# Three opening weight pieces on GpSimd's queue, and block-sum scalings behind the first eight tiles

## The chip, the cores and the metric

The kernel runs on one core of a Trainium2 chip. A core has engines that work side by side, each through its own list of instructions in order: TensorE (PE, the matmuls, with its weight loads listed as PEld), VectorE (DVE), ScalarE (ACT), GpSimd (POOL) and SyncE (SP), which here only issues transfers. A transfer (DMA) is issued by an engine's queue and carried out by the core's 16 DMA engines; a semaphore tells when it has landed. The metric is the device time of one execution in microseconds (us).

## The reference

One layer of a hybrid decoder: 16 learned meta tokens stand ahead of 2048 tokens of width 1024, all are RMS-normalised, projected by one matrix of 1024 x 4096 into eight groups, and go through a gated short convolution and a retention; an output projection, the residual and a last norm follow.

```python
def mixer_layer(h, norm_g, w_in, conv_w, ret_norm_g, w_out, pos):
    hn = rms_norm(h, norm_g)
    proj = jnp.einsum('bld,de->ble', hn, w_in)
    cx, cb, cc, cg, q, k, v, rg = jnp.split(proj, N_PROJ, axis=-1)
    conv_out = short_conv_branch(cx, cb, cc, conv_w) * jax.nn.silu(cg)
...
    ret = head_group_norm(retention_chunkwise(qf, kf, vf), ret_norm_g)
    ret_out = ret.astype(h.dtype) * jax.nn.silu(rg)
    mixed = jnp.concatenate([conv_out, ret_out], axis=-1)
    return h + jnp.einsum('ble,ed->bld', mixed, w_out)
```

## The kernel before

**Products in parts.** Matmuls run on rounded float32 (`F32R`). Each operand is split into a rounded high part (`mh`, `wh`, made by ScalarE) and the rest as a low part (`ml`, `wl`, made by VectorE), and each product is three matmuls: high by high, high by low, low by high. `split` (line 108) does this; with a scale, for the x tiles and their norm gain, ScalarE's line is 115 and VectorE's 116, without one they are 112 and 113.

**Tiles.** x comes transposed in tiles of 128 x 512 (`xT`, 256 KB each). For the first half of the sequence there are two groups `j` of 512 tokens, with eight tiles `k` of 128 model dimensions each. A set of weights is four blocks of 128 x 512: `n = 0, 1` make one output, `n = 2, 3` the other, and even `n` serve tiles 0 to 3, odd `n` tiles 4 to 7. Within a block, columns `128 k` to `128 (k+1)` belong to tile `k`. Later units use a scheme with seven products on sums of blocks (`quad`, line 236); the first unit is done plainly (`quad_plain`, matmuls on line 293): two outputs, three matmuls, so six matmuls to a tile of x.

**The opening.** Blocks 0 and 2 of the first set are cut in two `PIECES`: the first 128 columns, which tile 0 needs, and the other 384. Before, the two first pieces (64 KB each) were issued by ScalarE's queue on line 942, behind the small `gain`, and the two others (192 KB each) by SP's queue on line 990, behind x tile 0. Their casts and low parts are lines 999 and 1000. `moving` (line 167) loads and splits the x tiles in order and calls what stands for `(j, k)` in its dictionary `after`: `begin(0)` behind tile 0, `begin(1)` behind tile 3, which loads blocks 1 and 3 whole (line 498 issues them), and `normalise_meta` behind tile 7.

**Block sums.** The seven-product scheme wants sums of x blocks. `block_sums` starts with a scaling of one block by the gain on ScalarE (line 192), four in this stage, and goes on with VectorE's line 189 and a subtraction on GpSimd.

**Identity.** `make_identity` writes a 128 x 128 identity with two GpSimd instructions (`masks.py:197` and `199`), among the first of that engine. Its first reader is VectorE's line 314.

**What sets the order.** A planner takes the program, simulates it, and writes each engine's list. `tc.issue_after(ins)` makes instructions of the block that are on the same engine as `ins` stand behind it in that engine's list. It orders the list alone; nothing waits for `ins` to end. Waits come from data and from buffers.

Of the kernel before, what the change touches and what calls it, by code (L numbers as in the profile page):

```python
# [8 lines left out]
F32 = mybir.dt.float32  # L9
# [4 lines left out]
ALU = mybir.AluOpType  # L14
# [5 lines left out]
KT = D // P  # L20
NG = 4
# [5 lines left out]
KH = KT // 2  # L27
# [5 lines left out]
BLOCK = ((0, 7), (1, 5))  # L33
FIRST_W, PLAIN_W, B12 = 2, 3, 4
# [44 lines left out]
def hybrid_trunk(ctx: ExitStack, tc: tile.TileContext, t, out: bass.AP, chunk_decay):  # L79
# [5 lines left out]
    nc = tc.nc  # L85
# [18 lines left out]
    def brief(name="b"):  # L104
        return sb.tile([P, HB + 128], F32, name=name, tag="b", bufs=BRIEF)[:, :HB]

    lowered, fifth = [None], [None]

    def split(hi, lo, src, scale=None, eng=nc.vector):

        if scale is None:
            nc.scalar.copy(out=hi, in_=src)  # L112
            lowered[0] = eng.tensor_tensor(out=lo, in0=src, in1=hi.bitcast(F32), op=ALU.subtract)  # L113
            return
        nc.scalar.mul(hi, src, scale)  # L115
        nc.vector.scalar_tensor_tensor(
            out=lo, in0=src, scalar=scale, in1=hi.bitcast(F32), op0=ALU.mult, op1=ALU.subtract
        )
# [37 lines left out]
    def operand(i, kt):  # L156
        slot = B12 if i == 7 else i
        hi = sb.tile([P, HB], F32R, name=f"mh{i}{kt}", tag=f"mh{slot}{kt}", bufs=1)
        lo = sb.tile([P, HB], F32R, name=f"ml{i}{kt}", tag=f"ml{slot}{kt}", bufs=1)
        return hi, lo  # L160

    def parts(m, i, kt, src, factor=None):
        hi, lo = operand(i, kt)
        split(hi, lo, src, factor)
        m[i].append((hi, lo))

    def moving(load, scale=None, after={}):


        m = [[] for _ in range(8)]  # L170
        blocks = []
        for j in range(2):
            for half in range(2):
                for kt in range(KH):
                    k = half * KH + kt
                    blocks.append(load(k, j))
                    parts(m, BLOCK[half][j], kt, blocks[-1], scale(k) if scale else None)
                    after.get((j, k), lambda: None)()
        return m, blocks

# [165 lines left out]
    ident = const.tile([P, P], F32, name="ident")  # L346
# [67 lines left out]
    def gain_of(k):  # L414
        return gain[:, k : k + 1]

    def load_x(r):
        def load(k, j):
            a = gen("x")[:, :HB]
            nc.sync.dma_start(a, t["xT"][r, j, k])  # L420
            return a

        return load
# [514 lines left out]

    PIECES = slice(0, P), slice(P, HB)
    opening = {n: raw() for n in (0, 2)}  # L940
    for n, a in opening.items():
        nc.scalar.dma_start(a[:, PIECES[0]], t["w_in"][2 * NG, n][:, PIECES[0]])
    make_identity(nc, ident)
    nc.gpsimd.memset(ones, 1.0)
    nc.gpsimd.memset(neg_half, -0.5)
    nc.vector.tensor_copy(out=ones_r, in_=ones)
# [24 lines left out]
    for r in range(NR):  # L971
        f = factors[r]
        rot_t = sb.tile([P, 2, BLK], F32, name="rot_t", tag="rot_t", bufs=1)
        p0 = NMETA + r * BLK

        def load_tables():
            nc.sync.dma_start(rot_t, t["rot"][:, :, p0 : p0 + BLK])

        if r == 0:
            w = [None] * 4  # L980
            loads = w_loads(2 * NG)

            def begin(half):
                if half:
                    for n in (1, 3):
                        w[n] = plain_part(n, loads[n], FIRST_W)
                    return
                for n, a in opening.items():
                    w[n] = a, operand(FIRST_W, n)
                    nc.sync.dma_start(a[:, PIECES[1]], t["w_in"][2 * NG, n][:, PIECES[1]])  # L990
                done = []
                for cs in PIECES:
                    with ExitStack() as behind:
                        for ins in done:
                            behind.enter_context(tc.issue_after(ins.ins))
                        for n, a in opening.items():
                            hi, lo = w[n][1]
                            done = [
                                nc.scalar.copy(out=hi[:, cs], in_=a[:, cs]),
                                nc.vector.tensor_tensor(  # L1000
                                    out=lo[:, cs], in0=a[:, cs], in1=hi[:, cs].bitcast(F32), op=ALU.subtract
                                ),
                            ]

            m, b = moving(
                load_x(r), gain_of, {(0, 0): lambda: begin(0), (0, KH - 1): lambda: begin(1), (0, KT - 1): normalise_meta}
            )
            first = [[p for a, p in w]]
            blocks = None, meta_products([a for a, p in w])
            first.append(plain_parts(w_loads(2 * NG + 1)))  # L1010
            load_tables()
            nc.sync.dma_start(cols, t["cols"])
            t3 = [a[:, i * HB : (i + 1) * HB] for a in (row_tile("t3", 1) for _ in range(2)) for i in range(2)]
            t1 = [brief("t1") if n < BRIEF else sb.tile([P, HB], F32, name="t1", tag="tc", bufs=COPIES) for n in range(KH)]
            for kt in range(KH):
                b11, b21, b12, b22 = (b[n * KH + kt] for n in range(4))
                block_sums(b11, b12, b22, b21, t1[kt], t3[kt], gain_of(kt), gain_of(KH + kt), nc.gpsimd)
                parts(m, 2, kt, b22)
                parts(m, 6, kt, b21)
            for _ in row_factors(0, f):  # L1020
                pass
            nc.sync.dma_start(causal, t["causal"])
            nc.sync.dma_start(conv_w, t["conv_w"])
            nc.sync.dma_start(ret_g, t["ret_norm_g"])

            def late_parts():
                for i, held in ((3, t1), (4, t3)):
                    for kt in range(KH):
                        parts(m, i, kt, held[kt])

            between = (), idle, idle
            later = prepare(load_x(1), sums_x, gain_of)
        else:
            m, b = moving(load_x(r), gain_of)
            first = [plain_parts(w_loads(0))]
            load_tables()
            prepared(m, sums_x, (1, 3))

            def rest_of_sums():
                prepared(m, sums_x, (0, 2))  # L1040
                with tc.issue_after(loaded[0].ins):
                    kept.pop()()

            between = (), rest_of_sums, idle
            blocks = None, None
            later = prepare(load_w_out, sums_w)
        factors_ahead[0] = row_factors(r + 1, factors[r + 1]) if r < NR - 1 else iter(())
        units = UNITS[r]
        turning = None
        special = (first, between)  # L1050
        for n, unit in enumerate(units):
            following = units[n + 1] if n + 1 < len(units) else None
            rest = lambda: ahead(r, following, early=n == 0)
            if r + n == 0:
                blocks, completion = group_plain(unit - NG, m, f, blocks[1], first, late_parts, rest)
                special = (), completion
            elif unit < NG:
                if turning is None:
                    turning = [row_tile(name, 1 - r) for name in ("apart", "across")]
                sums = later if unit in MAKES_SUMS[r] else iter(())  # L1060
                blocks = head(unit, r, m, rot_t, f, turning, blocks, rest, sums, *(special if unit == 0 else ()))
            else:
                if r == NR - 1 and following is None:
                    lent = sb.tile([P, 2, BLK], F32, name="held", tag="rot_t", bufs=1)
                    areas = [lent[:, 0], lent[:, 1], row_tile("held", 0), row_tile("held", 0)]
                    for i, a in enumerate(areas):
                        for j in range(2):
                            n, kt = 2 * (i // 2), i % 2 * 2 + j
                            held[n, kt] = a[:, j * HB : (j + 1) * HB]
                            nc.sync.dma_start(held[n, kt], sums_w[n, kt])  # L1070
                blocks = conv_group(unit - NG, r, m, f, blocks, rest, FACTOR_STEPS.get(unit, ()) if r == 0 else (), r == 0 and following is None)
                if unit in MAKES_SUMS[r]:
                    with tc.issue_after(taken[0].ins):
                        next(later, None)

    m, b = moving(load_w_out)
# [42 lines left out]
```

## Time and profile before

| what | us |
|---|---|
| median of 3 runs | 870.76 (869.86 to 871.42) |
| profiled execution | 871.07 |
| its span | 869.3 |
| TensorE busy | 857.9 |
| VectorE busy | 722.5 |
| ScalarE busy | 497.9 |
| GpSimd busy | 396.6 |

The span is the profiled part of an execution; 1.8 us of the execution lie outside it. Busy times are of the whole span. A timeline row gives the start in us from the span's beginning, the duration, the engine, the line, the operation, what it writes and reads, its shapes and count, and in brackets how long the engine stood idle before it and what ended that. A row with a count merges neighbours of one kind. Names with a q, such as SPq, are the queue of that engine, which issues transfers.

### The profile page before, as it was taken

The numbers are of one execution on the slowest core, as the hardware profiler recorded it, in microseconds if no ns is written. First come the engines' busy times: TensorE is split into PE (matmuls) and PEld (weight loads), VectorE is DVE, ScalarE is ACT, GpSimd is POOL, SyncE is SP. The second block draws the span as 40 slices with busy tenths as digits, with TensorE's granted clock in tenths as the row PEclk, the third lists the DMA queues.
The fourth block names the chain that finished last, engine by engine and source line by source line (L and its number), as shares of the span: only waits on it lengthen the run. The fifth ranks groups of instructions, "written<-read, shape, count | busy, mean of one in ns | idle before, by whom it ended". The sixth has DMA issues, their size and how long they took to land.

```text
span 869.3 us, 12705 instructions
## 1 busy us (share of the span) xinstructions
PE 857.9 (99%) x4216; PEld 704.7 (81%) x4216; DVE 722.5 (83%) x1194; ACT 497.9 (57%) x899; POOL 396.6 (46%) x286
## 2 busy tenths in 40 slices
PE   9999999999999999999999999999999999999996
PEld 6878887878787878788888888888888888788885
DVE  6899988888897977989789898988767799867663
ACT  8676548383845554848383747553333566545553
POOL 0663332322246654352233333355645445677773
PEclk9999999999999999999999999999999999999999
DMA  9724336363656633845264656647122584545441
GB/s 332 226 80 97 76 82 164 106 171 110 136 192 186 202 98 97 306 155 146 61 139 140 130 161 121 206 109 218 49 78 78 171 327 133 167 162 179 160 134 73
DMA packets 127219, 129.51 MB, mean 149 GB/s; under 512 B 58353, under 2 KB 75569, under 8 KB 127153
## 3 DMA queue, kind: packets, MB, share of 16 engines
q1 hardware_dynamic: 126576, 128.30, 50.0%
q8 instruction: 33, 0.54, 0.3%
q10 hardware_dynamic: 576, 0.40, 0.1%
q14 instruction: 34, 0.27, 0.1%
HBM read 90.91 MB, written 25.17 MB: 134 GB/s over the span
## 4 chain that ended last, share of the span: by engine, by line
PE 86%; DVE 3%; ACT 3%; issue 1%; DMA 1%; SPq 0%; POOLq 0%; POOL 0%; ACTq 0%; DVEq 0%
PE pj L236 73%; PE pj L293 5%; PE ms L822 2%; PE ms L811 2%; PE ms L821 2%; PE ms L798 2%; DVE ml L113 1%; PE ms L456 1%; ACT v L769 1%; ACT wh L112 1%; ACT v L766 1%; DVE wl L113 1%; DMA w<-in_w_out 1%; ACT tc L243 1%; DVE yo L121 0%
## 5 line engine op out<-in xcount | busy, mean ns | idle before, releaser
L236 PE MATMUL pj<-mh,wl 128*128 128x512 f32 x1008 | 397.2, 394 | 1.5 <-ACT tc L243 0.8
L236 PE MATMUL pj<-mh,wh 128*128 128x512 f32 x1008 | 393.0, 390 | 0.0
L236 PE MATMUL pj<-ml,wh 128*128 128x512 f32 x1008 | 392.7, 390 | 0.0
L112 ACT CAST wh<-ra 128x512 fp32r<-128x512 f32 x216 | 133.8, 620 | 245.2 <-PE pj L236 209.6
L113 DVE TENSOR_TENSOR wl<-ra,wh 128x512 fp32r<-128x512 f32 x216 | 194.4, 902 | 40.8 <-ACT wh L112 39.9
L236 PEld LDWEIGHTS pj<-mh,wl 128*128 128x128 f32 x1008 | 189.3, 188 | 45.5 <-ACT tc L243 3.9
L236 PEld LDWEIGHTS pj<-mh,wh 128*128 128x128 f32 x1008 | 189.3, 188 | 39.7
L236 PEld LDWEIGHTS pj<-ml,wh 128*128 128x128 f32 x1008 | 189.3, 188 | 37.5
L121 POOL TENSOR_TENSOR sa<-ra 128x512 f32<-128x512 f32 x36 | 53.0, 1473 | 104.7 <-DMA ra<-in_w_in 39.5
L124 POOL TENSOR_TENSOR ra<-sa,ra 128x512 f32<-128x512 f32 x36 | 53.9, 1497 | 91.8 <-DVE wl L113 88.8
L124 POOL TENSOR_TENSOR ra<-ra 128x512 f32<-128x512 f32 x36 | 59.1, 1643 | 49.4 <-PE ms L456 28.1
L151 POOL TENSOR_TENSOR ra<-ra 128x512 f32<-128x512 f32 x36 | 60.2, 1673 | 46.9 <-issue 37.1
L243 ACT COPY tc<-pj 128x512 f32<-128x512 f32 x108 | 62.7, 580 | 0.1
L293 PE MATMUL pj<-mh,mh 128*128 128x512 f32 x128 | 51.1, 400 | 0.7 <-ACT mh L115 0.6
L293 PE MATMUL pj<-mh,ml 128*128 128x512 f32 x128 | 50.1, 391 | 0.9 <-DVE ml L113 0.9
L293 PE MATMUL pj<-ml,mh 128*128 128x512 f32 x128 | 48.0, 392 | 0.0
L834 POOL TENSOR_TENSOR rp<-rs,neg_half 128x4 f32<-128x4 f32 x16 | 18.9, 1184 | 38.5 <-DVE rs L121 38.4
L596 POOL TENSOR_TENSOR c<-c,rr 128x512 f32<-128x512 f32 x14 | 24.9, 1778 | 24.3 <-DVE c L637 15.6
L897 DVE TENSOR_TENSOR yo<-pj,yo 128x512 f32<-128x512 f32 (+1 forms) x33 | 22.0, 671 | 16.2 <-PE pj L236 8.4
L908 POOL TENSOR_TENSOR z<-yo,final_g 128x512 f32<-128x512 f32 x16 | 26.8, 1675 | 18.6 <-DVE yo L897 18.6
L596 POOL TENSOR_TENSOR c<-c,tc 128x512 f32<-128x512 f32 x14 | 24.2, 1732 | 21.9 <-ACT tc L622 16.3
L112 ACT CAST wh<-sa 128x512 fp32r<-128x512 f32 x36 | 22.2, 617 | 15.0 <-PE pj L236 14.6
(153 smaller groups left out, 1218.9 us busy)
## 6 DMA issues: line engine op xcount, KB each, us to landing
ra<-in_w_in SPq DMA_DIRECT2D x126, 256.0 KB, 2.8
x<-in_xT SPq DMA_DIRECT2D x48, 256.0 KB, 4.9
w<-in_w_out SPq DMA_DIRECT2D x32, 256.0 KB, 4.7
ra<-mixed SPq DMA_DIRECT2D x32, 256.0 KB, 2.9
yo<-in_x SPq DMA_DIRECT2D x32, 256.0 KB, 4.9
ra<-in_x SPq DMA_DIRECT2D x16, 256.0 KB, 3.7
mixed<-c SPq DMA_DIRECT2D x16, 256.0 KB, 2.5
mixed<-qg SPq DMA_DIRECT2D x16, 256.0 KB, 2.4
```

The source lines that it names most:

```text
L112: nc.scalar.copy(out=hi, in_=src)
L113: lowered[0] = eng.tensor_tensor(out=lo, in0=src, in1=hi.bitcast(F32), op=ALU.subtract)
L121: eng.tensor_tensor(out=out, in0=a, in1=b, op=ALU.add)
L124: eng.tensor_tensor(out=out, in0=a, in1=b, op=ALU.subtract)
L151: summed[0] = nc.gpsimd.tensor_tensor(out=a12, in0=a12, in1=a11, op=ALU.subtract)
L236: nc.tensor.matmul(bank, a[:, ks], b, start=first and kt == 0 and n == 0, stop=kt == KH - 1 and n == 2, skip_group_check=not first,)
L243: copied[0] = nc.scalar.copy(out=c, in_=bank)
L293: nc.tensor.matmul(banks[i], a[:, ks], b, start=half + kt + n == 0, stop=half == 1 and kt == KH - 1 and n == 2,)
L596: eng.tensor_tensor(out=out, in0=a, in1=b, op=ALU.mult)
L834: nc.gpsimd.tensor_tensor(out=rp, in0=rs, in1=neg_half.rearrange("p (c a) -> p c a", a=1), op=ALU.pow)
L897: last[0] = nc.vector.tensor_tensor(out=y[:, cs], in0=pp[:, cs], in1=y[:, cs], op=ALU.add)
L908: nc.gpsimd.tensor_tensor(out=ys[i][j], in0=y, in1=final_g[:, j * HB : (j + 1) * HB], op=ALU.mult)
```

## The change

The three pieces other than block 0's first go to GpSimd's queue, in the order block 2 first piece, block 0 rest, block 2 rest, and the identity is made behind them. SP's queue then holds x tiles alone at the start. ScalarE's order is set: x tile 1 behind the cast of block 2's first piece, tiles 2 and 3 and blocks 1 and 3 behind the cast of block 2's rest. The four block-sum scalings of this stage stand behind the rounding of tile 7.

```diff
-    for n, a in opening.items():
-        nc.scalar.dma_start(a[:, PIECES[0]], t["w_in"][2 * NG, n][:, PIECES[0]])
-    make_identity(nc, ident)
+    by_pool = None
+    for cs in PIECES:
+        for n, a in opening.items():
+            with tc.issue_after(by_pool.ins) if by_pool else nullcontext():
+                queue = nc.gpsimd if n or cs.start else nc.scalar
+                fetched = queue.dma_start(a[:, cs], t["w_in"][2 * NG, n][:, cs])
+            by_pool = fetched if n or cs.start else None
+    by_pool = by_pool.ins
+    with tc.issue_after(by_pool):
+        make_identity(nc, ident)
...
-                    parts(m, BLOCK[half][j], kt, blocks[-1], scale(k) if scale else None)
+                    with tc.issue_after(behind[j, k]().ins) if (j, k) in behind else nullcontext():
+                        parts(m, BLOCK[half][j], kt, blocks[-1], scale(k) if scale else None)
...
+            def rest_of_tiles():
+                with tc.issue_after(pieces[1].ins):
                     for n in (1, 3):
                         w[n] = plain_part(n, loads[n], FIRST_W)
...
+            def piece(at):
+                cs = PIECES[at]
+                with tc.issue_after(scaled[0].ins):
+                    for n, a in opening.items():
+                        if at == 0:
+                            w[n] = a, operand(FIRST_W, n)
+                        hi, lo = w[n][1]
+                        cast = nc.scalar.copy(out=hi[:, cs], in_=a[:, cs])
+                        nc.vector.tensor_tensor(
+                            out=lo[:, cs], in0=a[:, cs], in1=hi[:, cs].bitcast(F32), op=ALU.subtract
+                        )
+                return cast
+
+            pieces = []
+            after = {
+                (0, 0): lambda: pieces.append(piece(0)),
+                (0, 1): lambda: pieces.append(piece(1)),
+                (0, KH - 1): rest_of_tiles,
+                (0, KT - 1): lambda: (pieces.append(scaled[0]), normalise_meta()),
+            }
+            m, b = moving(load_x(r), gain_of, after, {(0, 1): lambda: pieces[0], (0, 2): lambda: pieces[1], (0, 3): lambda: pieces[1]})
...
-                block_sums(b11, b12, b22, b21, t1[kt], t3[kt], gain_of(kt), gain_of(KH + kt), nc.gpsimd)
+                with tc.issue_after(pieces[2].ins):
+                    block_sums(b11, b12, b22, b21, t1[kt], t3[kt], gain_of(kt), gain_of(KH + kt), nc.gpsimd)
```

`scaled[0]` is set in `split` to ScalarE's last scaled rounding, that of the x tile just split.

More of the change, by code (lines that the diff above doesn't have):

```diff
@@ L105, in brief @@
         return sb.tile([P, HB + 128], F32, name=name, tag="b", bufs=BRIEF)[:, :HB]
-    lowered, fifth = [None], [None]
+    scaled, lowered, fifth = [None], [None], [None]
     def split(hi, lo, src, scale=None, eng=nc.vector):
@@ L114, in split @@
             return
-        nc.scalar.mul(hi, src, scale)
+        scaled[0] = nc.scalar.mul(hi, src, scale)
         nc.vector.scalar_tensor_tensor(
@@ L165, in parts, with moving @@
         m[i].append((hi, lo))
-    def moving(load, scale=None, after={}):
+    def moving(load, scale=None, after={}, behind={}):
         m = [[] for _ in range(8)]
@@ L981, in hybrid_trunk @@
             loads = w_loads(2 * NG)
-            def begin(half):
-                if half:
+            def rest_of_tiles():
+                with tc.issue_after(pieces[1].ins):
                     for n in (1, 3):
                         w[n] = plain_part(n, loads[n], FIRST_W)
[L987 to L1003, printed above, removed]
@@ L1005, in hybrid_trunk @@
-            m, b = moving(
-                load_x(r), gain_of, {(0, 0): lambda: begin(0), (0, KH - 1): lambda: begin(1), (0, KT - 1): normalise_meta}
-            )
+            def piece(at):
[10 more added lines that the diff above has]
+                return cast
```

## The prediction

> **What bounds the kernel now.** I read the page's totals first, then the chain that ended last, then the opening in the timeline, because the change touches nothing behind the first 13 us by design.
>
> ```profile
> PE 857.9 (99%) x4216; PEld 704.7 (81%) x4216; DVE 722.5 (83%) x1194; ACT 497.9 (57%) x899; POOL 396.6 (46%) x286
> PE 86%; DVE 3%; ACT 3%; issue 1%; DMA 1%; SPq 0%; POOLq 0%; POOL 0%; ACTq 0%; DVEq 0%
> ```
>
> TensorE is busy or ahead of everything for nearly the whole span, and 86% of the chain is its own work. So a microsecond that TensorE doesn't lose in the opening is a microsecond of the end, as long as nothing later was waiting for something else. Busy time hides short stalls, since matmuls overlap; the loss is read from start to start. This is the opening of TensorE (start, duration, form):
>
> ```profile
> 4.87 1.35 PE L293 MATMUL pj<-mh,mh 128*128 128x512 f32 x2
> 5.72 0.19 PEld L293 LDWEIGHTS pj<-mh,mh 128*128 128x128 f32 x1 [0.57 <-ACT mh L999]
> 6.07 0.39 PE L293 MATMUL pj<-mh,ml 128*128 128x512 f32 x1
> 6.29 0.39 PE L293 MATMUL pj<-ml,mh 128*128 128x512 f32 x1
> 6.52 0.40 PE L293 MATMUL pj<-mh,ml 128*128 128x512 f32 x1
> 6.76 0.39 PE L293 MATMUL pj<-ml,mh 128*128 128x512 f32 x1
> 7.79 0.50 PE L293 MATMUL pj<-mh,mh 128*128 128x512 f32 x1 [0.65 <-ACT mh L115]
> 8.13 0.40 PE L293 MATMUL pj<-mh,ml 128*128 128x512 f32 x1
> ...
> 11.55 0.61 PE L293 MATMUL pj<-ml,mh 128*128 128x512 f32 x2
> 12.07 0.50 PE L293 MATMUL pj<-mh,mh 128*128 128x512 f32 x1
> 12.40 0.39 PE L293 MATMUL pj<-mh,ml 128*128 128x512 f32 x1
> ```
>
> Unhindered, one starts 0.23 us after another (6.29, 6.52), six to a tile of x. Three places are slower. The second matmul starts with its weights at 5.72, 0.85 after the first: 0.62 lost, and the step behind a wait is 0.34 instead of 0.23, 0.11 more. The second tile starts at 7.79, 1.03 after 6.76: 0.80 lost and 0.11. The fifth tile starts at 12.07, 0.29 after the pair's second (0.23 behind 11.55): 0.06 and 0.11. **Sum 1.81 us**; this is what the change can win here.
>
> The releasers are all ScalarE, so I read its row next:
>
> ```profile
> 1.18 0.94 ACTq L942 DMA_DIRECT2D ra<-in_w_in  x2
> ...
> 3.84 0.72 ACT L115 ACTIVATE mh<-x,gain 128x512 fp32r<-128x512 f32 x1 [0.19 <-DMA gain<-in_norm_g]
> 4.52 0.30 ACT L999 CAST mh<-ra 128x128 fp32r<-128x128 f32 x1
> 5.37 1.13 ACT L999 CAST mh<-ra 128x128 fp32r<-128x128 f32 x3 [0.55 <-DMA ra<-in_w_in]
> 6.41 0.72 ACT L192 ACTIVATE x<-x,gain 128x512 f32<-128x512 f32 x1
> 7.04 2.02 ACT L115 ACTIVATE mh<-x,gain 128x512 fp32r<-128x512 f32 x3
> 9.02 0.62 ACT L112 CAST mh<-ra 128x512 fp32r<-128x512 f32 x1
> ...
> 11.92 0.71 ACT L192 ACTIVATE x<-x,gain 128x512 f32<-128x512 f32 x1
> ```
>
> The wait at 5.37 is for a weight piece (block 2, first 128 columns) to land. At 6.41 a block-sum scaling (L192) stands ahead of the second tile's rounding at 7.04, 0.63 us. The queue and the landings (last column: us from issue to landing; each row is its own narrow window; the x row is the tile issued at 2.12, the ACT row the second of its two):
>
> ```profile
> 0.74 0.40 SPq L420 DMA_DIRECT2D x<-in_xT  x1
> 1.19 0.89 SPq L990 DMA_DIRECT2D ra<-in_w_in  x2
> 2.12 2.04 SPq L420 DMA_DIRECT2D x<-in_xT  x3
> ```
>
> ```profile
> SPq L420 <- DMA gain<-in_norm_g: 0.8, 1, 0.8
> ```
>
> ```profile
> x<-in_xT SPq DMA_DIRECT2D x1, 256.0 KB, 4.1
> ra<-in_w_in ACTq DMA_DIRECT2D x1, 64.0 KB, 3.7
> ra<-in_w_in SPq DMA_DIRECT2D x1, 192.0 KB, 3.1
> ra<-in_w_in SPq DMA_DIRECT2D x1, 192.0 KB, 3.5
> ```
>
> The second x tile is issued at 2.12, behind two weight pieces, and lands at 6.2. Block 2's first piece is issued at 1.66 (second half of the 0.94 pair) and lands at 1.66+3.7 = 5.36, which is the 5.37 above. The fourth x tile stood 0.8 us in SP for a landing before it could be issued.
>
> **The change part by part.** *One issue leaves ACT's queue* (0.47 us, half of 0.94). ScalarE's first rounding waits for gain and x at 3.84 all the same: nothing.
>
> *Two pieces leave SP's queue, three come to Pool's.* The x tiles behind them are issued 0.89 us plus a gap earlier: the second at 1.19 instead of 2.12, so it lands at about 6.2-0.93 = 5.3. No row of this trace shows a DMA issued by Pool. What it takes there, P, is bounded below by an issue on the other queues (0.45 to 0.47) and above by the slowest small Pool operation:
>
> ```profile
> L309 POOL TENSOR_TENSOR rc<-rs_v,neg_half x5: 923/1020/1482, 16.6 to 342.8; 128x4 f32<-128x4 f32 x4, 16x1 f32<-16x1 f32 x1
> 0.73 0.20 POOL masks.py:197 MEMSET ident<- 128x128 f32 x1 [0.29 <-POOLq L1108]
> ```
>
> I take P = 1.0, near that row's median of 1.02, since Pool works small jobs at about that price; the ends are 0.45 and 1.48. Pool starts at 0.73. From the end of an issue to landing I take the rows above less their issue: 2.85 to 3.25 for 64 KB (3.3 and 3.7 less 0.45, mean 3.05), 2.7 to 3.1 for 192 KB (3.1 and 3.5 less 0.42, mean 2.9). Then block 2's first piece lands at 0.73+1.0+3.05 = 4.78, block 0's rest at 0.73+2.0+2.9 = 5.63, block 2's rest at 0.73+3.0+2.9 = 6.63.
>
> The Trainium skill, page "DMA: Bandwidth & Descriptors", section "Anatomy of one DMA — SWDGE (gpsimd) path", fits about 2.0 us plus bytes over 436e3 to a Pool-issued DMA. By it block 2's rest (196,608 bytes) would land at an estimated 3.73+2.45 = 6.2, and the sum below would grow by 0.4. No row here can show it, so I stay with the rows.
>
> *First tile.* Block 2's cast starts at 4.8 instead of 5.37. The second matmul followed its cast's start by 0.35, so it comes at 5.15: 0.58 won, and the tile ends at 5.15+0.34+4×0.23 = 6.41.
>
> *Second tile.* ScalarE's new order is x0, both first pieces, x1, both rests, then x2 and x3; the added orderings are issue order in one engine, not waits for an end, but whatever stands behind a late piece stands too: x1 behind block 2's first piece, and x2, x3 and blocks 1 and 3 behind block 2's rest, with VectorE's low parts and TensorE behind these. x1 is rounded from 5.3 to 5.95, block 0's rest from 5.95 to 6.46 (0.51, a third of the pieces' row at 5.37 being longer than the small ones), so the tile starts at about 6.5. Block 2's rest lands at 6.63, its cast ends at 7.14, its matmul starts at 7.2 instead of 6.73: a **new wait of 0.47**. The tile ends at 7.2+0.34+4×0.23 = 8.46. Before, the third tile started after 8.13+5×0.23 = 9.28. **Won here: 0.82.**
>
> *Fifth tile.* Four scalings leave ScalarE's first 13 us, 4×0.63 = 2.5 us, the last of them at 11.92 just behind the fifth tile's rounding. This tile's loss of 0.17 goes: 8.46+2×1.37 = 11.2 is when TensorE asks for it, and the wire has 0.7 us to make up:
>
> ```profile
> 2.50:3.50 1.00, 1.00 (x3) 0.30 (x2) 0.00 (x0) 0.99 (x2) 0.00 (x0) 1.00 1.01 353
> ...
> 5.50:6.50 1.00, 0.94 (x4) 0.67 (x4) 0.72 (x3) 1.00 (x4) 0.00 (x0) 1.00 1.13 277
> 6.50:7.50 1.00, 0.65 (x3) 0.19 (x1) 0.65 (x2) 1.00 (x3) 0.00 (x0) 1.00 0.85 299
> 7.50:8.50 1.00, 0.71 (x3) 0.62 (x4) 0.73 (x2) 1.00 (x3) 0.00 (x0) 1.00 1.09 313
> ...
> 9.50:10.50 1.00, 1.00 (x6) 0.83 (x5) 0.95 (x2) 1.00 (x3) 0.00 (x0) 1.00 1.07 393
> ```
>
> Last column is GB/s: 277 to 313 between 5.5 and 8.5 against 393 later, some 290 KB short, which a queue filled earlier closes.
>
> *Scalings later.* They now stand after the eighth tile, at about 12.5 to 15, ahead of the second eight tiles' rounding. That half's first matmul is the 49th: 4.87+48×0.23+1.81 = 17.7 at the earliest now, 16.7 with the gain, and one scaling's length of rounding ahead of it ends near 15.8: about 1 us of cover. Without it each scaling would cost 0.63.
>
> *Identity later.* Built behind three issues, at about 4; its first reader starts at 19.01, so 14 us of cover:
>
> ```profile
> 19.01 0.15 DVE L314 TENSOR_TENSOR rot<-ident,rc 16x16 f32<-16x16 f32 x1
> ```
>
> **Sum:** 0.82+0.17 = 0.99 of the 1.81. The profiled execution took 871.07 (span 869.3), 0.31 over the median of 870.76; off the median the forecast is **869.8**. With P = 0.45 block 2's rest lands at 4.98 and all 1.81 goes: 868.95. With P = 1.48 it lands at 8.07, the third tile starts at 9.90, 0.62 late, less 0.17: 871.2.
>
> **Rivals.** *Pool is quick and the next wait moves too.* The next place where TensorE waits is the second row-factor product:
>
> ```profile
> 50.79 0.39 PE L293 MATMUL pj<-ml,mh 128*128 128x512 f32 x1
> 51.25 1.12 PE L340 MATMUL ms<-rot,ones 128*128 128x512 f32 x2
> ```
>
> 0.46 from start to start, 0.23 lost, waiting for VectorE. If the earlier transfers pull that in as well, 1.81+0.23 = 2.04 go: **868.7**. For it: ScalarE and VectorE run ahead once the pieces are there. Against: it needs P near the lower end.
>
> *The gain is given back there.* If VectorE's product ahead of 51.25 stays where it is, TensorE comes 1 us early and waits: **870.8**. Against: the row loads ahead of it reuse the weights' raw buffers, which TensorE's meta products and ScalarE's squares release, so they move along.
>
> *The wire, not the queue, is the limit.* DMA share is already 1.01 at 2.5, so the same bytes land no earlier and block 2's first piece still comes at 5.37; only the scaling's 0.63 ahead of x1 is won: **870.1**. Against: the 277 GB/s. The Trainium skill, same page, section "Issuing engines are not separate DMA queues", says that all issuers share the same 16 engines and that spreading saves only issue time; the share of 1.01 agrees with it.
>
> *Pool's queue is the new bottleneck (the other side).* The place is the cast of block 2's rest: the third tile starts at 5.46+3P (8.46 at P = 1.0), against 9.28+0.17 today. From P = 1.33 the change loses, from 1.91 it loses over 1.74 us. At 2.37, twice the mean of Pool's small powers below, it costs 5.46+7.11-9.45 = 3.12: **873.9**. For it: Pool is slow where VectorE is busy. Against: VectorE is at 0.00 from 2.5 to 3.5 in the windows above, when the issues should be running.
>
> ```profile
> L834 POOL TENSOR_TENSOR rp<-rs,neg_half 128x4 f32<-128x4 f32 x16 | 18.9, 1184 | 38.5 <-DVE rs L121 38.4
> ```
>
> **How the numbers follow.** 0.2%, 1.74 us, is about what a measurement of this kernel tells from no change. Forecast 0.40, quick Pool 0.27, wire 0.12, given back 0.09, slow Pool 0.12. Only the quick case passes 1.74 downwards and only the slow one upwards: faster 0.27, same 0.61, slower 0.12. The range leaves out the slow case alone and takes in both ends of P, with 0.4 us on the upper and some 0.6 on the lower side for what the planner may reorder behind the opening: 868.3 to 871.6.
>
> **What would show it.** Right: three issues on Pool's queue about 1 us apart from 0.73; x1's rounding straight behind the cast of block 2's first piece; the second matmul at about 5.2, the third tile at about 8.5, no L192 before the eighth tile's L115. Wrong: issues of over 1.3 us, a cast of block 2's rest behind 8, a start-to-start gap at TensorE over 0.5 in the second tile, or a longer wait ahead of L340 near 50.

## The result, and the profile after

| | before | after |
|---|---|---|
| median (range), us | 870.79 (869.86 to 871.42), 6 runs | 874.77 (873.44 to 875.45), 6 runs |
| ratio to before, 95% interval | | 1.0038 (1.0028 to 1.0047) |
| profiled execution, us | 871.07 | 873.61 |
| its span, us | 869.3 | 871.8 |

The change costs about 3.3 us by the ratio, where a gain of 1 us was forecast. In the profiled executions it is 2.54, since that of after lies 1.16 under its median and that of before 0.28 over its own. What follows explains the 2.54; the rest is taken up at the end.

The page of after has the engines as busy as before:

```profile
PE 857.9 (98%) x4216; PEld 704.9 (81%) x4216; DVE 722.4 (83%) x1194; ACT 497.6 (57%) x899; POOL 392.0 (45%) x289
PE 83%; DVE 4%; ACT 3%; issue 1%; DMA 1%; SPq 0%; POOLq 0%; POOL 0%; ACTq 0%; DVEq 0%
```

TensorE is busy for the same 857.9 us, and its share of the chain fell from 86% to 83%: it waits more. Where, shows from start to start. Its opening in the timeline of after:

```profile
5.09 1.03 PE L294 MATMUL pj<-mh,mh 128*128 128x512 f32 x2
...
6.65 0.40 PE L294 MATMUL pj<-ml,mh 128*128 128x512 f32 x1
8.63 0.50 PE L294 MATMUL pj<-mh,mh 128*128 128x512 f32 x1 [1.58 <-ACT mh L1003]
9.22 0.50 PE L294 MATMUL pj<-mh,ml 128*128 128x512 f32 x1
...
10.54 0.62 PE L294 MATMUL pj<-mh,ml 128*128 128x512 f32 x2
```

The first tile gained nothing that lasts (its sixth matmul is at 6.65; 6.76 before), the second starts at 8.63 instead of 7.79, and the 13th matmul, which opens the third tile in before, is the second of the last pair (10.54+0.23), at 10.77 instead of 9.28. ScalarE's row in the same stretch says why:

```profile
4.74 0.53 ACT L1003 CAST mh<-ra 128x128 fp32r<-128x128 f32 x2 [0.24 <-DMA ra<-in_w_in]
5.17 0.72 ACT L115 ACTIVATE mh<-x,gain 128x512 fp32r<-128x512 f32 x1
8.06 0.51 ACT L1003 CAST mh<-ra 128x384 fp32r<-128x384 f32 x1 [2.17 <-DMA ra<-in_w_in]
9.02 0.51 ACT L1003 CAST mh<-ra 128x384 fp32r<-128x384 f32 x1 [0.44 <-DMA ra<-in_w_in]
9.44 1.33 ACT L115 ACTIVATE mh<-x,gain 128x512 fp32r<-128x512 f32 x2
```

x tile 1 is rounded at 5.17, 1.87 us earlier than before. Then ScalarE stands for the large weight pieces, which are cast at 8.06 and 9.02 (before at 5.6 and 6.0, inside the x3 row at 5.37). GpSimd's row and the landings (issue to landing in the last column):

```profile
1.32 1.82 POOL L947 DMA_DIRECT2D ra<-in_w_in  x3 [0.44 <-issue]
```

```profile
ra<-in_w_in POOLq DMA_DIRECT2D x2, 192.0 KB, 6.2
ra<-in_w_in ACTq DMA_DIRECT2D x1, 64.0 KB, 3.5
ra<-in_w_in POOLq DMA_DIRECT2D x1, 64.0 KB, 3.6
```

The three issues take 1.82 us together, 0.6 each. The small piece lands after 3.6 us like the others. The large pieces take 6.2 (6.0 and 6.4), 3.1 and 3.5 before.

The second loss is at 51 us. TensorE's second row-factor product, which followed 0.46 behind the matmul ahead of it:

```profile
51.59 0.39 PE L294 MATMUL pj<-mh,mh 128*128 128x512 f32 x1
53.74 1.12 PE L341 MATMUL ms<-rot,ones 128*128 128x512 f32 x2 [1.77 <-DVE rot L315]
```

From start to start it is 2.15 now. The product stands 2.49 later than before (51.25), and so does what it is made from: the row loads on SP, the squares of the rows on ScalarE, their sum, the power on GpSimd and `rot` on VectorE. Followed back, the first step that slipped is SP's row of loads into the raw buffers of the second weight set, before and after:

```profile
24.36 13.96 SPq L367 DMA_DIRECT2D ra<-in_x  x16
```

```profile
24.74 16.55 SPq L368 DMA_DIRECT2D ra<-in_x  x16
```

The first of the sixteen is 0.38 later, the last 3.0. SP's waits from 24 to 42 us (us in total, times, longest) name what held the first of them, before and after:

```profile
SPq L367 <- DVE ml L113: 4.9, 3, 3.9
```

```profile
SPq L368 <- DVE ml L113: 8.1, 4, 4.3
```

These are VectorE's low parts of that set, the last readers of those buffers. VectorE before, then after:

```profile
23.67 0.67 DVE L113 TENSOR_TENSOR ml<-ra,mh 128x512 fp32r<-128x512 f32 x1
24.27 0.73 DVE L189 SCALAR_TENSOR_TENSOR x<-x,gain,t 128x512 f32<-128x512 f32 x1
24.93 1.88 DVE L113 TENSOR_TENSOR ml<-ra,mh 128x512 fp32r<-128x512 f32 x3
```

```profile
24.04 0.67 DVE L113 TENSOR_TENSOR ml<-ra,mh 128x512 fp32r<-128x512 f32 x1
24.64 0.73 DVE L190 SCALAR_TENSOR_TENSOR x<-x,gain 128x512 f32<-128x512 f32 x1
25.31 0.67 DVE L535 TENSOR_TENSOR u<-pj,u 128x512 f32<-128x512 f32 x1
25.91 0.78 DVE L447 TENSOR_TENSOR state<-state,rm 128x128 f32<-128x128 f32 x1
26.61 1.78 DVE L113 TENSOR_TENSOR ml<-ra,mh 128x512 fp32r<-128x512 f32 x1
```

The second low part ends at 28.39 where it ended at 25.60 before. Two more operations stand ahead of it, and it takes 1.78 instead of 0.67. SP's next load follows at once:

```profile
28.42 0.33 SPq L368 DMA_DIRECT2D ra<-in_x  x1
```

What lies beside the slow operation is GpSimd's pair of block-sum subtractions, before and after:

```profile
23.88 8.12 POOL L124 TENSOR_TENSOR t<-x 128x512 f32<-128x512 f32 x2 [6.37 <-DVE x L189]
```

```profile
22.28 5.57 POOL L124 TENSOR_TENSOR t<-x 128x512 f32<-128x512 f32 x2 [5.11 <-ACT mh L112]
```

Such a pair takes anything from 3.0 to 10.0 us in the traces of this case, so one engine seems to stand in the other's way; the run that takes the pair away, below, tests it. In after the first ends at 26.54, 1.23 behind the start of `u` at 25.31, the one operation of that stretch that reads PSUM, and the second runs from 26.50 to 27.84, while the low part at 26.61 doesn't finish. Before, the same `u` had run at 22.41, ahead of the subtractions, and the first of these took 6.42, to 30.3, behind all four low parts.

The Trainium skill, page "SBUF — State Buffer", section "SBUF: two separate sides", says that a VectorE operation with two SBUF inputs and a GpSimd operation that reads SBUF take one shared pair of ports, and that the one that starts first holds it for its whole instruction while the other stands. The rows agree: 1.78 is the wait to 27.84 and the operation's own 0.6, and `u`, with one SBUF input, seems to be where GpSimd gets in. That `u` is needed for it isn't shown: in the run again, below, the collision comes ahead of `u`, at a block-sum step of VectorE (24.81, 1.79 instead of 0.73), and the second low part still ends at 28.51.

### The profile page after: what moved, and what is told of

Its sections match the earlier page's. It is cut to its first block, busy times and chain, and to the rows that moved or that the text cites. A ratio compares the mean times of both kernels' runs of the same rounds, so it can differ in the third digit from the quotient of the medians.

```text
span 871.8 us, 12714 instructions
## 1 busy us (share of the span) xinstructions
PE 857.9 (98%) x4216; PEld 704.9 (81%) x4216; DVE 722.4 (83%) x1194; ACT 497.6 (57%) x899; POOL 392.0 (45%) x289
## 4 chain that ended last, share of the span: by engine, by line
PE 83%; DVE 4%; ACT 3%; issue 1%; DMA 1%; SPq 0%; POOLq 0%; POOL 0%; ACTq 0%; DVEq 0%
PE pj L237 71%; PE pj L294 4%; PE ms L823 2%; PE ms L812 2%; PE ms L822 2%; PE ms L799 2%; DVE ml L113 1%; PE ms L457 1%; ACT wh L112 1%; DVE wl L113 1%; ACT v L767 1%; ACT v L770 1%; DMA w<-in_w_out 1%; ACT tc L244 1%; DMA x<-in_xT 1%
## 5 line engine op out<-in xcount | busy, mean ns | idle before, releaser
L113 DVE TENSOR_TENSOR wl<-ra,wh 128x512 fp32r<-128x512 f32 x216 | 196.7, 912 | 40.6 <-ACT wh L112 39.8
L294 PEld LDWEIGHTS pj<-mh,mh 128*128 128x128 f32 x128 | 24.2, 189 | 8.3 <-ACT mh L1003 2.6
```

The costliest lines, as they stand in the source:

```text
L294: nc.tensor.matmul(banks[i], a[:, ks], b, start=half + kt + n == 0, stop=half == 1 and kt == KH - 1 and n == 2,)
```

## The experiments

Medians are of several executions, intervals of the ratio to before in the same call (median of before 870.63 to 871.14). Where there is one execution, it is said.

**The changed kernel again.**

> The changed kernel once more, beside the others on one chip. Both theories: 873.4 to 875.5 us, about 3 to 4.5 above the kernel before. If its times fall in two groups again, the granted clock goes with them (0.998 or 0.999 for the shorter, 0.996 for the longer).

874.08, ratio 1.0038 (1.0026 to 1.0050). The loss stands, and so does its place: the second tile starts at 7.98, the 13th matmul at 11.00, and the last of the 192 plain matmuls of the first unit, behind the product, at 59.01 (59.04 in after, 56.09 before). The 97th, the first of the second weight set, is used below to read the opening alone: 31.36 (31.11 in after, 29.86 before). The five times don't fall in two groups (873.80 to 874.80, granted clock 0.997 to 0.999).

**The change cut in two.** First before with the queues and the identity alone, then before with the scalings alone:

```diff
-                    nc.sync.dma_start(a[:, PIECES[1]], t["w_in"][2 * NG, n][:, PIECES[1]])
+                queue = nc.gpsimd if n or cs.start else nc.scalar
+                fetched = queue.dma_start(a[:, cs], t["w_in"][2 * NG, n][:, cs])
```

> The kernel before with the queue change alone: three weight pieces on GpSimd's queue, no new order on ScalarE, scalings where they were. Theory A (the pieces land late beside the x tiles; everything follows from that): the rests land at 8 to 9 us again and the time is as long as the changed kernel's or longer, 873 to 876 us. Theory B (moving the scalings reorders VectorE, so the row loads come late and the second row-factor product waits): only the opening's loss of about 1.3 us, 872 us, and less than 1 us of wait ahead of the second row-factor product.

```diff
+(0, KT - 1): lambda: (eighth.append(scaled[0]), normalise_meta())
...
+                with tc.issue_after(eighth[0].ins):
+                    block_sums(b11, b12, b22, b21, t1[kt], t3[kt], gain_of(kt), gain_of(KH + kt), nc.gpsimd)
```

> The kernel before with the scalings alone moved behind the eighth tile. Theory A: the second tile's rounding comes 0.6 us earlier, 870.0 to 870.8 us, and the wait ahead of the second row-factor product stays under 0.5 us. Theory B: that wait grows to about 2 us and the time to about 872 us.

The queues alone give 874.04, 1.0038 (1.0026 to 1.0051): the whole loss. The large pieces land after 6.2 us there too, the second tile starts at 10.14, and nothing is lost at the product at 51 us: that run pays in the opening only. It pays more there than after does: the 97th matmul is at 34.21, 4.35 late, 1.7 of it through the clock (last section). 2.82 are left at the end of its profiled execution.

The scalings alone give 871.56, 1.0010 (1.0002 to 1.0019), not faster, although the opening did gain: the second tile starts at 7.21 (7.79) and the 192nd matmul at 54.93 (56.09), 1.16 earlier (0.83 at the 97th). It is lost again behind it, which neither theory expected, since the product doesn't wait here. The first place, TensorE in that run:

```profile
60.37 0.39 PE L236 MATMUL pj<-mh,wh 128*128 128x512 f32 x1
61.57 0.47 PE L236 MATMUL pj<-mh,wl 128*128 128x512 f32 x1 [0.81 <-DVE wl L113]
```

1.20 from start to start, waiting for the low part of a weight sum that VectorE reaches at 60.74, behind three operations of 1.7 to 1.8 us beside GpSimd's sums. Before, the same step takes 0.50, so 0.7 of the gain goes here; the rest goes at waits between 312 and 361 us, whose cause stays open.

**All of the change but the queues.**

```diff
-                queue = nc.gpsimd if n or cs.start else nc.scalar
-                fetched = queue.dma_start(a[:, cs], t["w_in"][2 * NG, n][:, cs])
+    for n, a in opening.items():
+        nc.scalar.dma_start(a[:, PIECES[0]], t["w_in"][2 * NG, n][:, PIECES[0]])
...
+            def rests():
+                for n, a in opening.items():
+                    nc.sync.dma_start(a[:, PIECES[1]], t["w_in"][2 * NG, n][:, PIECES[1]])
```

> The changed kernel with the four pieces on their old queues; ScalarE's new order and the moved scalings stay. Theory A: the rests land near 5 us, the second tile starts at about 6.9, the time is 869.0 to 870.5 us, under the kernel before. Theory B: the opening gains about 1 us, the second row-factor product waits 1.7 us longer, 871.5 to 872.5 us.

873.24, 1.0033 (1.0024 to 1.0043): ScalarE's fixed order costs without GpSimd's queue as well, and more than either theory allowed. With the pieces ahead of it on SP, x tile 1 lands late, and the order lets nothing else go first:

```profile
6.85 0.72 ACT L115 ACTIVATE mh<-x,gain 128x512 fp32r<-128x512 f32 x1 [1.22 <-DMA x<-in_xT]
```

Only 0.38 of it is left at the 97th matmul (30.24 to 29.86), but the product at 51 us waits here too, 51.63 to 53.41. By the ratios the queues alone cost 3.3 us, all but the queues 2.9, and both together 3.3. The costs don't add up, because the two parts act on each other: by the 97th matmul the queues alone lose 4.35, all but the queues 0.38, and both together 1.25. With the pieces on GpSimd's queue, the new order saves in the opening some of what it costs at the product.

**Why the large pieces land late.** All four pieces on ScalarE's queue (one execution); the changed kernel with x tile 2 held until both large pieces have landed (one execution); and the same with everything of SP behind that tile held as well (one execution):

```diff
+            nc.scalar.dma_start(a[:, cs], t["w_in"][2 * NG, n][:, cs])
```

> The changed kernel with all four pieces issued by ScalarE's queue instead of three by GpSimd's. The x tiles still go ahead on SP's queue. A1: two queues share again, so the rests take 5 us or more from issue to landing. A2: 3 to 4 us, as the rests on SP's queue did in the kernel before (3.1 and 3.5). ScalarE's first rounding starts near 4.7 instead of 3.8, behind two more issues.

```diff
+            if (r, j, k) == (0, 0, 2):
+                nc.gpsimd.tensor_copy(out=a[:, 0:1], in_=opening[0][:, HB - 1 : HB])
+                nc.gpsimd.tensor_copy(out=a[:, 1:2], in_=opening[2][:, HB - 1 : HB])
```

> The changed kernel with SP's third x tile and all behind it held until both rests from GpSimd's queue have landed. Theory A1 (the rests are slow because they share the DMA engines with the x tiles of SP's queue): issue to landing falls from 6.0 and 6.4 us to 3 to 4, both casts done by about 6.5. Theory A2 (a transfer issued by GpSimd is slow by itself): still 6 us or more. The time is no test here, since the x tiles come late: 873 to 877 us.

```diff
+        def load(a, i):
+            with tc.issue_after(third[0].ins) if third[0] is not None else nullcontext():
+                nc.sync.dma_start(a, t["w_in"][n, i])
```

> The changed kernel, except that SP issues nothing between the second x tile and the landing of both 192 KB weight pieces on GpSimd's queue: the third x tile waits for both to have landed, and the other early loads of SP stand behind it. Theory sharing (the pieces are slow because the x tiles share the DMA engines with them): the two 192 KB pieces land 3 to 4 us after their issue instead of 6.0 and 6.4. Theory GpSimd's queue (a transfer issued there is slow by itself): they still take 5 to 6 us. The total tells nothing, since x tiles 2 to 7 now come late: some 876 to 880 us.

On ScalarE's queue the large pieces take 5.0 and 3.8 us, between the two theories, and land at 7.14 and 7.47 instead of 8.04 and 9.00. The 97th matmul is at 29.90, where it was before. Yet the total is 874.26, that of after: the product at 51 us follows by 2.70. So the opening can be cured and the loss stay. The second run didn't settle it: other loads of SP went ahead in place of the held tile, so the DMA engines weren't clear, and the pieces took 5.0 (time 879.07). The third run cleared them. Its landings:

```profile
ra<-in_w_in POOLq DMA_DIRECT2D x2, 192.0 KB, 3.9
```

and ScalarE, which casts both at 6.08 instead of 8.06 and 9.02:

```profile
6.08 0.93 ACT L1016 CAST mh<-ra 128x384 fp32r<-128x384 f32 x2 [0.32 <-DMA ra<-in_w_in]
```

6.2 falls to 3.9 when two x tiles and four small loads stand beside the pieces, instead of four x tiles and two blocks. So 2.3 us of the late landing need the neighbours; what is left above the 3.3 of SP's queue before is 0.6. That the neighbours alone do it isn't shown: with the same four x tiles issued ahead on SP, ScalarE's queue took 5.0 and 3.8. There SP issued the two blocks 1.2 and 1.5 us later, so the run doesn't part the two causes; how much of the 2.3 is GpSimd's queue under load stays open. (The x tiles behind come late in that run, 874.23.) By the Trainium skill's fit for a GpSimd-issued transfer that the prediction quotes, page "DMA: Bandwidth & Descriptors", section "Anatomy of one DMA — SWDGE (gpsimd) path", 192 KB would take an estimated 2.45 us; the least that these runs show for one is 3.8.

**Why the product waits.** The scalings of the meta tokens (`state`) moved behind the low parts on VectorE; then GpSimd's subtractions moved behind its first power; then both, and `u` behind the low parts too:

```diff
+            with tc.issue_after(lowered[0].ins):
+                pieces[3]()
```

> The changed kernel with the two multiplications that finish the meta tokens placed behind the low parts of the second set of weights on VectorE. Theory C (the second row-factor product waits because those low parts free the raw buffers of the row loads, and they end at 28.4 to 30.3 instead of 25.6 to 26.8): the row loads start earlier, the wait ahead of that product falls from 1.9 us to about 1, the time by about 1 us, to 873.2. Rival D (the row loads are late for another reason, the opening's own delay): no change, 874.2 us.

```diff
+            differences.append(lambda: sub(eng, t3, b22, b11))
...
+                if n == CH + 1:
+                    with tc.issue_after(powered[0].ins):
+                        while differences:
+                            differences.pop(0)()
```

> The changed kernel, except that GpSimd's four block-sum subtractions of the first unit stand behind its first power for the row factors. Theory collision (the subtraction runs on GpSimd beside VectorE's low parts of the second weight set, whose buffers SP's row loads wait for): the four low parts take 0.67 us each instead of up to 1.78, the last sixteen row loads are issued 1.5 us or more earlier, TensorE's second row-factor product follows its forerunner by 0.6 us or less instead of 2.16, and the time is 872.6 to 873.2. Rival (something else holds the row loads, or the same loss shows at the next wait): the product moves but the total stays at 874.1, within 0.3.

```diff
+                with tc.issue_after(second[0].ins) if second else nullcontext():
+                    mul(nc.vector, s, pp, s)
```

> As the run with GpSimd's subtractions held back, and besides VectorE's first product out of PSUM (u) and the two scalings of the meta tokens stand behind the low parts of the second weight set. Theory order (what is left of the wait at TensorE's second row-factor product, 1.35 us with the subtractions held back, is that those operations stand between the low parts): the last low part ends 0.7 us earlier, near 27.7, the product follows its forerunner by 0.5 to 0.8 us, and the time is 872.0 to 872.3; with the opening's loss of about 1.0 us left, it stays above the kernel before. Rival (the wait is set by something else, such as the squares or the row loads' transfers): the low parts end earlier, the product stays at 52.4 to 52.8, and the time at 872.7.

The first is a miss: 874.02, 1.0032 (1.0020 to 1.0044), the product at 53.92. The small operation went, and the collision hit its neighbours, 1.19 and 1.78 for a low part and a block-sum step of VectorE (L190).

The second hits: 872.75, 1.0027 (1.0016 to 1.0037), 1.3 us under the run of after again by the medians, 1.0 by the ratios, whose intervals overlap; so the trace has to carry it. VectorE and TensorE in it:

```profile
25.06 0.67 DVE L538 TENSOR_TENSOR u<-pj,u 128x512 f32<-128x512 f32 x1
25.66 0.27 DVE L450 TENSOR_TENSOR state<-state,rm 128x128 f32<-128x128 f32 x1
25.86 0.67 DVE L113 TENSOR_TENSOR ml<-ra,mh 128x512 fp32r<-128x512 f32 x1
```

```profile
51.35 0.39 PE L297 MATMUL pj<-mh,mh 128*128 128x512 f32 x1
52.70 0.70 PE L344 MATMUL ms<-rot,ones 128*128 128x512 f32 x1 [0.96 <-DVE rot L318]
```

With nothing of GpSimd beside it the low part takes 0.67 and ends 1.86 earlier, and the product is 1.04 earlier. Of both, some 0.24 was there ahead of it: `u` starts at 25.06 instead of 25.31, and the 97th matmul is at 30.87 instead of 31.11. The step at the product falls from 2.15 to 1.35, and the collision is shown as a cause of these 0.80. But the product still waits 1.35, more than the 0.6 that was expected.

The third was to show that the order of VectorE's list is the rest, and its theory fell. The low parts end at 27.98 as expected (30.26 in after), and the time is 875.74, 1.0054 (1.0041 to 1.0067), the slowest of all with intervals. GpSimd, VectorE and TensorE in it:

```profile
44.46 8.91 POOL L124 TENSOR_TENSOR t<-x 128x512 f32<-128x512 f32 x2 [2.64 <-DVE x L190]
53.33 1.27 POOL L121 TENSOR_TENSOR sa<-ra 128x512 f32<-128x512 f32 x1
54.55 1.03 POOL L313 TENSOR_TENSOR rc<-rs_v,neg_half 128x4 f32<-128x4 f32 x1
```

```profile
50.28 0.67 DVE L542 TENSOR_TENSOR u<-u,rr 128x512 f32<-128x512 f32 x1
55.61 0.69 DVE L318 TENSOR_TENSOR rot<-ident,rc 128x512 f32<-128x512 f32 x1 [4.67 <-POOL rc L313]
```

```profile
52.38 0.39 PE L297 MATMUL pj<-mh,mh 128*128 128x512 f32 x1
56.36 1.22 PE L344 MATMUL ms<-rot,ones 128*128 128x512 f32 x1 [3.60 <-DVE rot L318]
```

Here GpSimd is the one that stands. The first of its next pair of subtractions begins at 44.46 and ends at 52.10, 1.15 behind the point at which VectorE has run dry (50.28+0.67), and the power that the product needs (L313) is behind it in GpSimd's list: 3.98 us at TensorE. The clock fell to half behind it for 6.83 us, so the profiled execution, 878.21, lies 2.5 above the median. The squares had ended at 45.9, 2.2 ahead of after's. The same collision thus cuts both ways; what decides which engine loses isn't shown.

**The product moved.** If the loss is TensorE standing at this product, it should go when the product stands behind the products for the meta tokens:

```diff
+                def rest_and_rows():
+                    made = rest()
+                    with tc.issue_after(multiplied[0].ins):
+                        for _ in row_steps:
+                            pass
+                    return made
```

> The changed kernel, with only the second row-factor product put on TensorE behind the first unit's products for the meta tokens, as in the run with the scalings. Theory (the changed kernel loses about 1.0 us in the opening and the rest by TensorE standing still for this product): the wait of 2.16 us ahead of it goes, and the time is 872.0 to 872.8. Rival (what the product is made of is needed just as much by what follows it, so the wait turns up at the next user): no wait at the product but 873.6 to 874.3 all the same.

872.98, 1.0022 (1.0013 to 1.0032): 1.1 us under the run of after again, 1.4 by the ratios, a little above the 872.0 to 872.8 that was expected. The product follows within 0.23 and waits for nothing. What is left, 1.3 at the 192nd matmul against the same edit on before (56.21 and 54.88), is the opening. Of the 2.15 us at the product, a step of 0.23 is no loss, 0.23 was lost before as well, and 0.41 is won back behind it (below); the 1.28 left agree with the 1.1 to 1.4.

**Better than both.** The scalings behind x tile 1 only; before with the product moved; and before with the scalings behind tile 7 and the product moved:

```diff
+(0, 1): lambda: eighth.append(scaled[0])
```

> The kernel before with the scalings held only behind the rounding of x tile 1, in place of tile 7; queues and the rest untouched. If what the scalings alone gained in the opening (1.2 us at the 192nd matmul) was given back by a changed order hundreds of microseconds later, this one, whose later order is that of the kernel before, keeps about 0.6 to 0.9 us: 869.8 to 870.1 us. If the gain is an accident of the profile: 870.6 us, no change.

> The kernel before, with only the second row-factor product put behind the first unit's products for the meta tokens: the control for the run with the scalings. Expected 870.4 to 870.9 if the product's place matters only where the opening is quicker; below 870.0 if the wait at the product costs by itself.

> The kernel before, with the scalings behind the eighth x tile, and the second row-factor product put on TensorE behind the first unit's products for the meta tokens. If the 1.17 us won in the opening by the scalings alone is lost at 60 us because GpSimd's weight sums start behind TensorE's product, the wait of 0.8 us for VectorE's low part at 61 us goes and the time is 869.5 to 870.2. Rival (TensorE meets another wait whatever the order, because VectorE's and GpSimd's lists are what is late there): 870.8 to 871.6.

The first is 871.03, 0.9999 (0.9990 to 1.0008), no gain: in its profile the second tile starts only 0.16 earlier, as block 2's first piece is cast at 5.49 (5.37 before), and the fifth tile, behind scalings that now stand between, starts at 12.26 (12.07 before). The second is 870.50, 1.0000 (0.9992 to 1.0008): the product's place alone is worth nothing. Both together are 870.25, 0.9990 (0.9981 to 0.9999). TensorE at the moved product:

```profile
54.17 0.39 PE L293 MATMUL pj<-ml,mh 128*128 128x512 f32 x1
54.40 1.02 PE L340 MATMUL ms<-rot,ones 128*128 128x512 f32 x2
```

GpSimd's weight sums now run from 46.95 to 54.5, where with the scalings alone they ran from 47.13 to 60.3, and the wait of 0.81 at 61 us doesn't come. It is the one version that is faster than both, by some 0.9 us (0.1 to 1.7) by the ratio, 0.5 by the medians, with no weight piece on GpSimd's queue. It is one of eleven with an interval, and this one only just stays below 1.

## Why the prediction was wrong

**The bound, not reached.** Of the 1.81 us of the opening, the scalings alone won 0.85 by the 49th matmul, and with the product moved 1.01; no run won more. That all of it could be won isn't shown.

**P, wrong to the good.** An issue on GpSimd takes 0.6 us; 1.0 was taken, 0.45 to 1.48 allowed.

**The landings, the step that failed.** "From the end of an issue to landing I take the rows above": 2.9 us for 192 KB was a duration of SP's queue at a place behind one x tile. After the change the same bytes stand beside four x tiles and two more blocks, issued by SP between 0.75 and 3.5. From the end of their issue the large pieces took 5.4 and 5.9. Cast of block 2's rest: 6.63 forecast, 9.02 measured; with the measured issues (end at 3.14) and 2.9 it would have been 6.04. The run with the wire clear gives back 2.3 of it. The forecast thus counted an earlier x tile as a gain and not as a load on the transfers that it overtakes, and took SP's duration for GpSimd's queue. The prediction had named a cast of block 2's rest behind 8 and a longer wait near 50 as signs of being wrong; both came.

**"A queue filled earlier closes" the 290 KB, right in part, and no help.** Over the 5.5 to 8.5 us of the prediction the mean rate is 296 GB/s before, 336 in after and 393 in the run again, which closes the gap. In after a fall stands ahead, to 205 and 270 where before has 332 and 277; again, with 308 and 373, doesn't have it, and why is open:

```profile
4.50:5.50 1.00, 1.00 (x4) 0.45 (x3) 0.97 (x3) 0.76 (x3) 0.00 (x0) 1.00 1.35 205
5.50:6.50 1.00, 1.00 (x5) 0.78 (x5) 0.75 (x2) 0.39 (x1) 0.00 (x0) 1.00 0.74 270
```

So it isn't the rate that makes the pieces late: in the run again block 2's rest lands at 9.21 with the gap closed. More bytes move, and others land first.

**The rivals.** "The wire, not the queue, is the limit" came nearest in cause, as far as the clear wire shows it, with the wrong price: it reckoned that nothing lands earlier and not that the pieces land later. The slow queue had the right place, the cast of block 2's rest, and the right sign there: the 13th matmul is 1.49 late, 1.25 of it left at the 97th. Its cause, P, was wrong, and its 873.9 is near the total by luck: it puts at one place what came of two.

**"They move along", the second step that failed.** The rival that gives the gain back at the second row-factor product was set aside because TensorE and ScalarE release the row loads' buffers. VectorE's low parts release the first of them, as SP's waits show, and after the shift two other operations and a subtraction of GpSimd came ahead of the second of these. That is 1.7 us in the profiled execution (the 192nd matmul is 2.95 late, the 97th 1.25), of which 0.80 is the collision at 26 us by the run that took it away. The 192nd's 2.95 falls to 2.54 at the end: 0.41 net are won back behind it, mostly from waits that before has there, such as the 0.26 at 61.5.

**"A microsecond that TensorE doesn't lose in the opening is a microsecond of the end", wrong for gains.** The scalings won 1.16 and kept none. A loss is kept better than a gain, since a later wait catches an early engine and helps a late one only by its own slack: of the 2.95 of after 2.54 are left, of the 4.35 of the queues alone 2.82.

**Open.** The medians differ by 1.4 us more than the profiled executions, the ratio by 0.8. The clock described below may be part of that: of the six executions of after, the three at a mean granted clock of 0.998 or 0.999 took 873.44 to 874.32, the three at 0.996 took 875.21 to 875.45. It isn't all, since the run again has no execution at 0.996 and the same ratio. How much of the late landing is GpSimd's queue and how much its neighbours wasn't parted. What of the remaining 1.35 us at the product, with the first collision gone, is VectorE's order and what the second collision wasn't separated: the run made for it moved the second collision too.

## What to carry to other kernels

A transfer that is put ahead of others takes from those that it overtakes: price the overtaken ones with the new neighbours, not with the duration that they had. When work moves by a few microseconds, look at the waits up to the next point where all engines meet, and list there which operations of VectorE and GpSimd come to lie beside each other. Take a gain in an opening as a gain only when the next wait of the critical engine moves too.

## What the runs showed of the hardware

A GpSimd subtraction of 128 x 512 takes 1.3 us at its quickest and up to 8.4 beside VectorE, and a VectorE operation of 0.67 takes 1.78 beside it.

TensorE's granted clock fell to half after some short standstills. With the queues alone, behind a step of 2.41 us (7.73 to 10.14), and with the pieces on ScalarE's queue, behind 2.70 at the product, the windows show (third from last is the clock):

```profile
11.20:14.40 3.20, 3.20 (x8) 2.55 (x9) 2.48 (x6) 3.20 (x7) 0.00 (x0) 0.50 1.06 391
```

```profile
52.40:55.60 3.20, 3.20 (x31) 1.40 (x34) 3.20 (x7) 2.24 (x5) 0.00 (x0) 0.50 0.00 0
```

Each lasts 3.41 us in the trace, which costs TensorE 1.7 us. Behind the 3.98 of the slowest run it lasted 6.83. Behind the 2.15 of after it didn't happen in its profiled execution, nor behind a step of 2.72 (62.78 to 65.50) in the run with the wire clear. A wait of some two microseconds and a half can thus be paid nearly twice; what decides it, these runs don't show.
